# The two meta rows of a projection, as fp32 matmuls on four column tiles of the array

## The chip, the core and the metric

The kernel runs on one core of a Trainium2 chip. The metric is the time of one execution on the device in microseconds (us); lower is better. The core has the matrix engine TensorE (PE in the profile, with its weight loads listed as PEld), the vector engine (DVE), the scalar engine (ACT), GpSimd (POOL) and SyncE (SP), which here issues most DMAs. Each engine works through its own instructions in their order; engines wait for one another by semaphores.

## The reference, cut to what matters

One layer of a hybrid decoder: 1024 tokens of width 1024, with 16 meta tokens put ahead of them. Two branches (attention and convolution) are merged under gates into `mixed`, and the step that the change touches is the product of `mixed` with `w_out` and the normalisation behind it:

```python
mixed = jax.nn.sigmoid(g_attn) * y_attn + jax.nn.sigmoid(g_conv) * y_conv
h = layer_norm(DEEPNORM_ALPHA * h + mixed @ w_out, ln1_g, ln1_b)
up = causal_dwconv(h @ ffn_w_up, ffn_dw, ffn_dw_b)        # 3 taps, causal
...
return h[:, N_META:]
```

Everything is float32. The meta tokens are dropped at the end, but the causal convolution over 3 tokens reads the two tokens ahead of the first real one. So the last two meta rows of `h` are needed, and only these two.

## The kernel before, in words

**Precision.** A float32 product is made of three faster ones in the type `float32r`: each operand is split into a high part, its value in that type, and a low part, what is left. `product` (L340, L343, L344) issues three matmuls per piece of 128 input channels: low x high, high x high, high x low. ACT makes the high parts and DVE the low ones (`split`, L300 and L303).

**The stage around the change.** `w_out` has 8 blocks of 128 rows, k = 0 to 7. `prep_wo` loads a block as float32 (the raw block) and splits it into `wo[k]`, a high and a low part. The raw blocks 0 to 3 lie in the buffer `FA` (columns 2064, 3088, 0 and 1024 on, each 1024 wide), 4 in `FA` from 4112, 5 in `OB` from 3072, and 6 and 7 in `wraw`, a ring of two buffers whose next users are the raw weights `w_up` of the following stage. Once a raw block is split, its place is free.

`out_rows(i)` computes the rows of token tile i (128 tokens): two halves of 512 output columns, 24 matmuls each, into a PSUM tile `ps_w` (tag `mm`, three buffers in turn). DVE adds the residual row, loaded by SP from `h0d` (L1345), collects statistics (L1346) and normalises (L1369). `turn` transposes the rows of an earlier tile on PE (L1379), and ACT writes them scaled into `FA` or, for edge rows, into `edge`. The tiles are taken in the order 3, -1, 7, 2, 6, 0, 4, 1, 5. The tile -1 is the pair of meta rows; the transposes of a tile stand between the halves of the next one, and those of the pair stand after the first half of tile 2.

**The pair.** When the branches are merged, for each block m the two columns of `mixed` that belong to the two meta tokens are written into `pair`: high parts by ACT in `pair[:, m, 0:2]` (L1187), low parts by DVE in `pair[:, m, 2:4]` (L1188). In `out_rows(-1)` each half takes 16 matmuls: per block one with all four columns against the high part of `w_out` (L1356), and one with the two high columns against its low part (L1357). Both add into partitions 0 to 3 of one PSUM tile. ACT copies these four rows out (L1358). Then the rows 2 and 3, which come from the low parts, are moved by a DMA to partitions 0 and 1 and added by DVE (L1364); so are the two residual rows from `h0d` (L1362).

**Order.** A scheduler places every engine's instructions by ranks and by its own estimate of time. `after(a, b)` fixes that a comes behind b in the order of work, without a semaphore. In the kernel before nothing fixes where the pair's matmuls stand; they lie partly between those of tile 3.

Of the kernel before, what the change touches and what calls it, by code (L numbers as in the profile page):

```python
# [23 lines left out]
F = mybir.dt.float32  # L24
R = mybir.dt.float32r
AF = mybir.ActivationFunctionType
OP = mybir.AluOpType
AX = mybir.AxisListType

P = 128  # L30
D = 1024
KC = D // P
# [81 lines left out]
def tile_hybrid_layer(  # L114
# [3 lines left out]
    nc = tc.nc  # L118
# [5 lines left out]
    def load(o, i):  # L124
        return nc.sync.dma_start(out=o, in_=i)
# [5 lines left out]
    def f32(ap):  # L131
        return ap.bitcast(F)

    def after(ins, first):

        tc.add_manual_dep(ins.ins, first.ins.name, mybir.DependencyInfo(
            mybir.DependencyClass.NoSync, mybir.DependencyReason.SCHED_ONLY), reason="order of work")
# [10 lines left out]
    const = ctx.enter_context(tc.tile_pool(name="const", bufs=1, side="left"))  # L148
# [8 lines left out]
    FA = arena.tile([P, 6144], F, name="FA")  # L157
    RHC = arena.tile([P, KC * T], R, name="RHC")
    RHO = arena.tile([P, KC * T], R, name="RHO")
    OB = arena.tile([P, 4 * U], F, name="OB")  # L160
# [8 lines left out]
    h0d = dpool.tile([U, D], F, name="h0d")  # L169
# [11 lines left out]
    start = ExitStack()  # L181
# [30 lines left out]
    tc.cur_priority = RK_START  # L212
    n_right, n_kept = COLS[2][0], COLS[-1][0]
    colr = constr.tile([P, n_right], F, name="colr")
    coll = const.tile([P, n_kept - n_right + 24], F, name="coll")[:, :n_kept - n_right]
    with rank(12):
        load(coll, cols_in[:, n_right:n_kept])
        load(colr, cols_in[:, :n_right])
# [117 lines left out]
    def product(ps, terms, behind=None):  # L336

        n = len(terms)
        for i, (ah, al, bh, bl) in enumerate(terms):
            ins = nc.tensor.matmul(ps, al, bh, start=i == 0, stop=False)  # L340
            if i == 0 and behind is not None:
                after(ins, behind)
            nc.tensor.matmul(ps, ah, bh, start=False, stop=False)  # L343
            last = nc.tensor.matmul(ps, ah, bl, start=False, stop=i == n - 1)  # L344
        return last
# [159 lines left out]
    turned, tms = {}, {}  # L505
# [87 lines left out]
    for a, b in ((0, 400), (400, J_LEN)):  # L593
        ps = pat.tile([P, 512], F, name="ps_v", tag="o" if a == 0 else "mm", bufs=1 if a == 0 else 3)
# [204 lines left out]
    ps = pat.tile([P, 512], F, name="ps_vm", tag="t", bufs=2)  # L799
# [34 lines left out]
    for h in range(NH):  # L834
        g, r = divmod(h, 4)
# [282 lines left out]
    def mixed(i, k, hl):  # L1118
        t, j = MX_AT[i]
        o = j * 2048 + (k * 2 + hl) * P  # L1120
        return t[:, o:o + P]
# [7 lines left out]
        return t[:, 0:8192].rearrange("p (t j x) -> p t j x", t=2, j=2)[:, :, j, cols]  # L1129

    w_out_v = w_out.rearrange("(k p) c -> k p c", p=P)
    wo = {}

    def prep_wo(k, raw=None, behind=None):
        if k < 4:
            hi, lo = (OA[:, OA_WO + k * 2048 + x:OA_WO + k * 2048 + x + 1024] for x in (0, 1024))
        elif k < 6:
            hi, lo = ((RX[:, RX_WO:], RW)[k - 4][:, x:x + 1024] for x in (0, 1024))
        else:
            hi, lo = wsp_flat()  # L1140
        if raw is None:
            raw = wraw([P, D])
            load(raw, w_out_v[k])
        split(raw, hi, lo, behind)
        wo[k] = (hi, lo)

    pair = const.tile([P, KC, 4], R, name="pair")
    g_next = [0]

    GS = [(FA, i * 516) for i in range(4)]  # L1150
# [11 lines left out]
    for m in range(KC):  # L1162
        hi, lo = weights([P, KC, P], lambda raw: load(raw, w_ab[m]))

        def branch(i, g, tag, bufs):
            a, b = PG[g]
            ps = pat.tile([P, 512], F, name="ps_p", tag=tag, bufs=bufs)
            rhs = (oo, conv)[i]
            for k in range(4):
                ah, al = hi[:, 4 * i + k], lo[:, 4 * i + k]  # L1170
                for j, (x, hl) in enumerate(((ah, 0), (ah, 1), (al, 0))):
                    nc.tensor.matmul(ps[:, :b - a], x, rhs(k, hl, a, b), start=k + j == 0, stop=k == 3 and j == 2)  # L1172
            return ps[:, :b - a]

        def merge(g, psa, psb):
            a, b = PG[g]
            n = b - a
            with rank(RK_EVAC):
                t = gslot()[:, :, :n]
                ins = load(t, dram(sgd, m * P * U + a, [[U, P], [KC * P * U, 2], [1, n]]))  # L1180

                ta, tb = t[:, 0], t[:, 1]
                nc.vector.scalar_tensor_tensor(ta, ta, 1.0, psa, OP.add, OP.mult)
                nc.vector.scalar_tensor_tensor(tb, tb, 1.0, psb, OP.add, OP.mult)
                nc.vector.tensor_tensor(ta, ta, tb, OP.add)
                if g == 0:
                    nc.scalar.mul(pair[:, m, 0:2], ta[:, 0:2], 0.5)  # L1187
                    nc.vector.scalar_tensor_tensor(pair[:, m, 2:4], ta[:, 0:2], 0.5, f32(pair[:, m, 0:2]),  # L1188
                                                   OP.mult, OP.subtract)
                v = ta[:, n - 256:].rearrange("p (t x) -> p t x", t=2)  # L1190
                h = mixed2(g, m, 0)
                last_act = nc.scalar.mul(h, v, 0.5)
                nc.vector.scalar_tensor_tensor(mixed2(g, m, 1), v, 0.5, f32(h), OP.mult, OP.subtract)
            return ins, last_act

        if m < KC - 1:
            pa = [branch(0, g, "mm", 3) for g in range(2)]
            for g in range(4):
                if g > 1:
                    pa.append(branch(0, g, "mm", 3))  # L1200
                last_gate, last_act = merge(g, pa[g], branch(1, g, "t", 2))
        else:
            pa = [branch(0, g, "mm", 3) if g < 3 else branch(0, g, "s", 2) for g in range(4)]
            for g in range(4):
                last_gate, last_act = merge(g, pa[g], branch(1, g, "t", 2))
        if m in (2, 3):
            raw = (FA[:, 4112:5136], OB[:, 3072:4096])[m - 2]
            load(raw, w_out_v[m + 2])
            prep_wo(m + 2, raw, last_act)
        if m < 4:  # L1210
            early.append(FA[:, E_AT[m]:E_AT[m] + 1024])
            after(load(early[m], w_out_v[m]), last_gate)
# [104 lines left out]

    WO_ORDER = (4, 5, 0, 1, 2, 3, 6, 7)
    edge = const.tile([P, 2, KC, 2], F, name="edge")
    r_next = [1]  # L1320

    def out_rows(i, between=(), work=()):


        n, u = (P, 2 + i * P) if i >= 0 else (2, 0)
        if n == P:
            o = r_next[0] % 2 * 1024
            r_next[0] += 1
            whole = RT[:, o:o + 1024]
            load(whole, h0d[u:u + n, :])  # L1330
        else:
            whole = OB[:, 3072:4096]
        r = whole[:n]
        order = WO_ORDER if i != 5 else (0, 1, 2, 3, 6, 7, 4, 5)
        turned = None
        st = small.tile([P, 2, 6], F, name="st")
        pin = line if i in (0, 4, 1, 5) else lambda ins: ins
        for half in range(2):
            hs = slice(half * 512, half * 512 + 512)
            ps = pat.tile([P, 512], F, name="ps_w", tag="mm", bufs=3)  # L1340
            if n == P:
                last = product(ps, [(mixed(i, k, 0), mixed(i, k, 1), wo[k][0][:, hs], wo[k][1][:, hs])
                                    for k in order], turned)
                with rank(RK_TURN):
                    pin(nc.vector.tensor_tensor(r[:, hs], ps, r[:, hs], OP.add))  # L1345
                    pin(nc.vector.bn_stats(st[:, half], r[:, hs]))  # L1346
                turned = None
                if len(between) > half:
                    turned = turn(*between[half], behind=[last])
                if half == 0:  # L1350
                    for f, *x in work:
                        f(*x)
                continue

            for j, k in enumerate(order):
                nc.tensor.matmul(ps[:4], pair[:, k], wo[k][0][:, hs], start=j == 0, stop=False)  # L1356
                last = nc.tensor.matmul(ps[:2], pair[:, k, 0:2], wo[k][1][:, hs], start=False, stop=j == KC - 1)  # L1357
            nc.scalar.copy(whole[:4, hs], ps[:4])  # L1358
        if n < P:
            q = FA[:4, 0:1024]  # L1360
            load(q[0:2], h0d[0:2, :])
            nc.vector.tensor_tensor(r, r, q[0:2], OP.add)  # L1362
            load(q[0:2], whole[2:4])
            nc.vector.tensor_tensor(r, r, q[0:2], OP.add)  # L1364
        with rank(RK_TURN):
            (mu, rs), = ln_stats([(r, n)], half_stats=st if n == P else None)
            for a in (512, 0) if i == 5 else (None,):
                x = r if a is None else r[:, a:a + 512]
                ins = pin(nc.vector.tensor_scalar(x, x, mu, rs, OP.subtract, OP.mult))  # L1369
        if n == P:  # L1370
            load(h1d[u - 2:u - 2 + P, :], r)
        return whole, n, ins
# [520 lines left out]
```

## Time and profile before

| | |
|---|---|
| median of 3 runs (lowest to highest) | 1255.88 us (1255.16 to 1256.59) |
| span of the profiled execution, first to last instruction | 1253.2 us |
| time of that execution beyond its span | not given by the profile |
| mean granted TensorE clock | 0.999 |
| matmuls of the pair | 32, from 510.3 to 518.8 us |
| HBM read and written | 150.29 MB and 62.70 MB |

How to read the rows that follow: a timeline row has the start, the duration, the engine, the line of the kernel, the operation, the output and its inputs by the program's names, the shape and the count. For a matmul "128*4 128x512" is the stationary operand (128 rows, 4 columns) and the moving one (128 partitions, 512 elements). Matmuls are pipelined, so durations overlap and their spacing is the difference of two starts. Brackets at the end of a row say how long the engine was idle ahead of it and who released it. A row of a line or tile has the count, then minimum, median and maximum duration in ns, then the first and last start.

### The profile page before, as it was taken

To read this page: it belongs to the slowest core of one execution; us is meant where nothing else is said; L and a number is where in the kernel's file an instruction comes from. 1 tells how busy PE (TensorE), PEld (TensorE's weight loads), DVE (VectorE), ACT (ScalarE), POOL (GpSimd) and SP (SyncE) were. 2 spreads that over 40 slices of the span, in tenths; PEclk is the share of its full clock that TensorE was granted. 3 is DMA by queue.
4 is the path that set the end of the run, shared out by engine and by line. 5 is a ranking of instruction groups with operands and counts; after the bars stand their busy time and mean duration, and the time that the engine had idled before them with its cause. 6 is when DMAs were issued, how large, how long until landed. Compare 5 with 4: busy or idle time off the path is not lost.

```text
span 1253.2 us, 23194 instructions
## 1 busy us (share of the span) xinstructions
PE 1239.1 (99%) x9176; PEld 1173.8 (94%) x9176; DVE 1078.1 (86%) x1862; ACT 627.4 (50%) x1284; POOL 7.4 (1%) x8
## 2 busy tenths in 40 slices
PE   8999999999999999999999999999999999999997
PEld 7999999999999999788899999999999998888886
DVE  8989999999978677448899999998999977896697
ACT  8533255655474233344676556565565654545330
POOL 0000000001000000000000000000000000000000
PEclk9999999999999999999999999999999999999999
DMA  7383633432256564222145555453454567998712
GB/s 261 117 292 102 191 93 98 109 95 81 73 157 173 170 164 119 85 94 75 68 160 191 194 197 201 161 211 137 163 206 175 196 227 251 395 342 330 276 60 84
DMA packets 98687, 212.20 MB, mean 169 GB/s; under 512 B 11395, under 2 KB 38595, under 8 KB 98322
## 3 DMA queue, kind: packets, MB, share of 16 engines
q1 hardware_dynamic: 84414, 199.57, 46.9%
q10 hardware_dynamic: 14164, 11.15, 2.8%
q8 instruction: 72, 1.18, 0.4%
q14 instruction: 37, 0.30, 0.1%
HBM read 150.29 MB, written 62.70 MB: 170 GB/s over the span
## 4 chain that ended last, share of the span: by engine, by line
PE 96%; DVE 2%; ACT 1%; DMA 1%; issue 0%; SPq 0%; DVEq 0%; ACTq 0%
PE px L1594 15%; PE py L1594 10%; PE ps_x L1739 9%; PE ps_z L340 8%; PE ps_z L343 8%; PE ps_z L344 8%; PE ps_z L1739 7%; PE ps_p L1172 7%; PE pz L1594 5%; PE pw L1594 5%; PE ps_w L344 2%; PE ps_w L343 2%; PE ps_w L340 2%; PE ps_z L575 2%; PE ps_t L943 1%; PE ps_s L919 1%
## 5 line engine op out<-in xcount | busy, mean ns | idle before, releaser
L340 PE MATMUL ps_z<-RHO,w 128*128 128x256 f32 (+2 forms) x864 | 243.2, 281 | 0.0
L343 PE MATMUL ps_z<-RHO,w 128*128 128x256 f32 (+2 forms) x864 | 242.3, 280 | 0.0
L344 PE MATMUL ps_z<-RHC,w 128*128 128x256 f32 (+2 forms) x864 | 242.2, 280 | 0.0
L343 PEld LDWEIGHTS ps_z<-RHO,w 128*128 128x128 f32 x864 | 162.5, 188 | 0.5
L344 PEld LDWEIGHTS ps_z<-RHC,w 128*128 128x128 f32 x864 | 162.7, 188 | 0.2
L340 PEld LDWEIGHTS ps_z<-RHO,w 128*128 128x128 f32 x864 | 162.5, 188 | 0.1
L749 DVE SCALAR_TENSOR_TENSOR FA<-cin,cdw,FA 128x1026 f32<-128x1026 f32 x120 | 154.3, 1295 | 0.7
L300 ACT CAST w<-wr 128x1024 fp32r<-128x1024 f32 x37 | 38.8, 1048 | 64.0 <-PE ps_z L344 48.0
L1412 DVE TENSOR_TENSOR RHO<-wr,RHO 128x512 fp32r<-128x512 f32 x94 | 64.0, 684 | 3.6 <-ACT RHO L1411 3.5
L1411 ACT CAST RHO<-wr 128x512 fp32r<-128x512 f32 x94 | 56.9, 619 | 15.6 <-DVE wr L1429 7.9
L1429 DVE TENSOR_TENSOR wr<-wr 128x512 f32<-128x512 f32 x88 | 60.1, 683 | 0.1
L758 ACT ACTIVATE FA<-ps_z,colr 128x258 f32<-128x258 f32 (+1 forms) x64 | 30.1, 472 | 59.0 <-PE ps_z L344 50.7
L303 DVE TENSOR_TENSOR w<-wr,w 128x1024 fp32r<-128x1024 f32 x37 | 45.1, 1218 | 7.6 <-ACT w L300 7.4
L1606 ACT COPY FA<-px 128x516 f32<-128x516 f32 (+2 forms) x23 | 13.1, 571 | 71.2 <-PE px L1594 71.2
L1172 PE MATMUL ps_p<-OC,w 128*128 128x256 f32 (+1 forms) x384 | 48.1, 278 | 0.0
L1172 PE MATMUL ps_p<-OA,w 128*128 128x256 f32 (+1 forms) x384 | 47.8, 278 | 0.0
L1172 PEld LDWEIGHTS ps_p<-OC,w 128*128 128x128 f32 x384 | 46.2, 188 | 0.1
L1172 PEld LDWEIGHTS ps_p<-OA,w 128*128 128x128 f32 x384 | 45.9, 188 | 0.0
L1412 DVE TENSOR_TENSOR w<-wr,w 128x512 fp32r<-128x512 f32 x60 | 40.7, 684 | 4.7 <-ACT w L1411 4.7
L1594 PE MATMUL px<-OA,RHO 128*128 128x260 f32 x324 | 43.0, 282 | 0.0
L1594 PE MATMUL px<-OC,RHO 128*128 128x256 f32 x324 | 41.2, 276 | 0.8 <-DVE OB L1345 0.8
L1594 PE MATMUL px<-RHC,RHO 128*128 128x256 f32 (+1 forms) x312 | 40.6, 279 | 0.1
(457 smaller groups left out, 3109.3 us busy)
## 6 DMA issues: line engine op xcount, KB each, us to landing
wr<-in_w_up_dram SPq DMA_DIRECT2D x44, 512.0 KB, 3.6
wr<-in_w_z_dram SPq DMA_DIRECT2D x29, 512.0 KB, 4.2
OB<-in_w_down_dram SPq DMA_DIRECT2D x24, 512.0 KB, 5.2
fd<-FA SPq DMA_DIRECT2D x44, 256.0 KB, 2.0
FA<-sd SPq DMA_DIRECT2D x15, 512.0 KB, 8.9
qt<-qd SPq DMA_DIRECT2D x28, 256.0 KB, 4.1
OB<-td SPq DMA_DIRECT2D x14, 512.0 KB, 8.7
sgd<-FA ACTq DMA_DIRECT2D x48, 128.0 KB, 2.4
```

The source lines that it names most:

```text
L300: ins = nc.scalar.copy(hi, raw)
L303: return nc.vector.tensor_tensor(lo, raw, f32(hi), OP.subtract)
L340: ins = nc.tensor.matmul(ps, al, bh, start=i == 0, stop=False)
L343: nc.tensor.matmul(ps, ah, bh, start=False, stop=False)
L344: last = nc.tensor.matmul(ps, ah, bl, start=False, stop=i == n - 1)
L749: nc.vector.scalar_tensor_tensor(acc[c], cin[:, j:j + U], wc, acc[c], OP.mult, OP.add)
L1172: nc.tensor.matmul(ps[:, :b - a], x, rhs(k, hl, a, b), start=k + j == 0, stop=k == 3 and j == 2)
L1411: nc.scalar.copy(hi, src)
L1412: ins = nc.vector.tensor_tensor(lo, src, f32(hi), OP.subtract)
L1429: ins = nc.vector.tensor_tensor(*x)
L1594: ins = nc.tensor.matmul(o, (ah, ah, al)[j][:, k * P:(k + 1) * P], bmat(sub, q, j, k), start=first and i == 0, stop=i == 11, skip_group_ch ...
L1739: nc.tensor.matmul(banks[i], l[:, ts], r[:, ws], start=first and a and x + k == 0, stop=z and x == len(ops) - 1 and k == 2, skip_group_che ...
```

## The change

The pair's product is computed from unsplit float32 operands. `pair` becomes a float32 tile of 2 x 8 columns, two per block, followed by 32 columns of zeros. The low parts (L1188) are no longer computed. For block k the stationary operand is the 32 columns from 2k on, of which the first two are the pair's and the rest are not used afterwards; the moving operand is the raw block of `w_out`. Block k writes the partitions from 32 x (k mod 4) on: the four groups of 32 partitions belong to four column tiles of the array, and each of them adds up two blocks. A half takes 8 matmuls, 16 in all. They stand in one row behind tile 3 and ahead of tile 7: each is placed behind the one before by `after`, and so is the first matmul of each token tile's half, unless a transpose stands ahead of it.

ACT copies all 128 partitions out. Then the residual rows and the partial sums in partitions 32, 64 and 96 are moved to partitions 0 and 1 by four DMAs, in two slots of `FA` in turn, and added by four DVE operations. The raw blocks of `w_out` stay in use until the row, so the pair's rows lie in `OB` from 2048 instead of 3072, where raw block 5 is. The padding of `coll` shrinks by as many columns as `pair` grows (16).

```diff
-    coll = const.tile([P, n_kept - n_right + 24], F, name="coll")[:, :n_kept - n_right]
+    coll = const.tile([P, n_kept - n_right + 8], F, name="coll")[:, :n_kept - n_right]
...
-        wo[k] = (hi, lo)
-
-    pair = const.tile([P, KC, 4], R, name="pair")
+        wo[k], wo_raw[k] = (hi, lo), raw
+
+    pair = const.tile([P, 2 * KC + 32], F, name="pair")
+    nc.vector.memset(pair[:, 2 * KC:], 0.0)
...
-                    nc.scalar.mul(pair[:, m, 0:2], ta[:, 0:2], 0.5)
-                    nc.vector.scalar_tensor_tensor(pair[:, m, 2:4], ta[:, 0:2], 0.5, f32(pair[:, m, 0:2]),
-                                                   OP.mult, OP.subtract)
+                    nc.scalar.mul(pair[:, 2 * m:2 * m + 2], ta[:, 0:2], 0.5)
...
-            whole = OB[:, 3072:4096]
+            whole = OB[:, 2048:3072]
...
+                behind = turned or (w_last[-1] if w_last else None)
                 last = product(ps, [(mixed(i, k, 0), mixed(i, k, 1), wo[k][0][:, hs], wo[k][1][:, hs])
-                                    for k in order], turned)
+                                    for k in order], behind)
+                w_last.append(last)
...
-            for j, k in enumerate(order):
-                nc.tensor.matmul(ps[:4], pair[:, k], wo[k][0][:, hs], start=j == 0, stop=False)
-                last = nc.tensor.matmul(ps[:2], pair[:, k, 0:2], wo[k][1][:, hs], start=False, stop=j == KC - 1)
-            nc.scalar.copy(whole[:4, hs], ps[:4])
+            for k in range(KC):
+                o = k % 4 * 32
+                last = nc.tensor.matmul(ps[o:o + 32], pair[:, 2 * k:2 * k + 32], wo_raw[k][:, hs], start=k < 4,
+                                        stop=k >= 4)
+                after(last, w_last[-1])
+                w_last.append(last)
+            nc.scalar.copy(whole[:, hs], ps)
         if n < P:
-            q = FA[:4, 0:1024]
-            load(q[0:2], h0d[0:2, :])
-            nc.vector.tensor_tensor(r, r, q[0:2], OP.add)
-            load(q[0:2], whole[2:4])
-            nc.vector.tensor_tensor(r, r, q[0:2], OP.add)
+            for j, src in enumerate((h0d[0:2, :], whole[32:34], whole[64:66], whole[96:98])):
+                q = FA[:2, j % 2 * 1024:j % 2 * 1024 + 1024]
+                load(q, src)
+                nc.vector.tensor_tensor(r, r, q, OP.add)
```

More of the change, by code (lines that the diff above doesn't have):

```diff
@@ L1131, in tile_hybrid_layer @@
     w_out_v = w_out.rearrange("(k p) c -> k p c", p=P)
-    wo = {}
+    wo, wo_raw = {}, {}
     def prep_wo(k, raw=None, behind=None):
@@ L1319, in tile_hybrid_layer @@
     edge = const.tile([P, 2, KC, 2], F, name="edge")
-    r_next = [1]
+    r_next, w_last = [1], []
     def out_rows(i, between=(), work=()):
```

## The prediction

> **What bounds the kernel now.** I read the busy shares and the chain that ended last on the page, then the waits of PE, then the timeline of PE around the row of the two meta tokens, and last the engines and queues that feed or empty that row.
>
> ```profile
> PE 1239.1 (99%) x9176; PEld 1173.8 (94%) x9176; DVE 1078.1 (86%) x1862; ACT 627.4 (50%) x1284; POOL 7.4 (1%) x8
> PEclk9999999999999999999999999999999999999999
> PE 96%; DVE 2%; ACT 1%; DMA 1%; issue 0%; SPq 0%; DVEq 0%; ACTq 0%
> PE pw L1594 <- ACT FA L1392: 1.2, 1, 1.2
> PE px L1594 <- DVE OB L1345: 0.8, 1, 0.8
> 620.00:900.00 280.00, 280.00 (x2415) 280.00 (x2414) 262.03 (x421) 171.50 (x369) 0.00 (x0) 1.00 0.49 177
> ```
>
> TensorE (PE) is busy for 99% of the span at the full granted clock and carries 96% of the chain. The two wait rows are all that PE waits for after 506 us: 2.0 us, both on the last token tile, whose date is set by PE itself. The windows row (PE, PEld, DVE, ACT, POOL busy, then clock and DMA) shows the next stage: DVE is nearly full, 262 of 280 us, but PE does not wait for it. So what PE gains or loses in the changed row should reach the end one for one, unless a feeder of that row turns late.
>
> The row itself, in the timeline (start, duration, engine, line):
>
> ```profile
> 510.05 0.39 PE L344 MATMUL ps_w<-w,RHC 128*128 128x512 f32 x1
> 510.27 0.40 PE L1356 MATMUL ps_w<-RX,pair 128*4 128x512 f32 x1
> ...
> 513.05 0.39 PE L1356 MATMUL ps_w<-OA,pair 128*4 128x512 f32 x1
> ...
> 518.84 0.40 PE L1357 MATMUL ps_w<-w,pair 128*2 128x512 f32 x1
> 519.08 0.40 PE L340 MATMUL ps_w<-RX,RHC 128*128 128x512 f32 x1
> ...
> 524.56 1.03 PE L1379 MATMUL ps_h<-coll,OB 128*128 128x128 f32 x8
> 510.05:519.08 9.03, 7.75 (x32) 2.70 (x32) 0.00 (x0) 0.00 (x0) 1.00 0.29 107
> ```
>
> Durations overlap, so cost is read from start to start. From 513.05 to 519.08 there are 26 matmuls of the row in 6.03 us, 0.232 us each. From 519.08 to 524.56 there are the 24 matmuls of half a token tile in 5.48 us, 0.228 us each. The last line is the window cut to the tile `pair`: all 32 matmuls of the row start in it, and seven of token tile 3 besides. **Removed: 32 x 0.232 = 7.42 us** of PE; the seven belong to tile 3 and stay.
>
> **The change part by part.** *The new matmuls.* Sixteen fp32 matmuls, stationary 32 columns, moving 512 columns; the trace has no fp32 matmul on several column tiles, but it has fp32 matmuls:
>
> ```profile
> L572 PE MATMUL ps_z<-FA,wr x32: 392/393/497, 12.6 to 21.2; 128*128 128x272 f32 x32
> 15.89 5.67 PE L572 MATMUL ps_z<-FA,wr 128*128 128x272 f32 x24
> 21.40 0.82 PE L518 MATMUL ps_h<-coll,xn 128*128 128x128 f32 x6
> 8.33 0.09 PEld L595 LDWEIGHTS ps_v<-tab 128*8 128x8 f32 x1 [0.25 <-issue]
> 8.66 0.09 PEld L595 LDWEIGHTS ps_v<-tab 128*8 128x8 f32 x1 [0.24 <-issue]
> ```
>
> The code issues 16 matmuls at L572, and the trace has 32: each fp32 matmul is **two passes**, one right behind the other on the same part of the array. 24 passes of 272 columns take 21.40 - 15.89 = 5.51 us, 0.2296 us each, or 0.844 ns per column; the passes of 400 columns at L595 (8 stationary columns) are 0.33 us apart, 0.83 ns per column. The present row needs 0.232 / 512 = 0.45 ns. So a pass over 512 columns is an estimated 512 x 0.844 = **0.432 us**, and 16 matmuls have 32 of them. What that costs hangs on how many run side by side; no row shows that, so I bound it:
>
> - nothing overlaps: 32 x 0.432 = 13.8 us, +6.4 us against 7.42;
> - all four tiles run at once: 8 x 0.432 = 3.5 us, -4.0 us;
> - between them: tiles are independent, but passes start in the order of the program. The order is tile 0 first pass, tile 0 second pass, tile 1 first pass, and so on. Tile 0's second pass must wait for its first, and tile 1's first pass stands behind it. It then starts beside it. Two passes run at any time, each matmul costs one pass, and the row is 17 x 0.432 = 7.35 us, **-0.1 us**.
>
> I take the last one: the timeline of PE nowhere shows a matmul overtaking another, and L572 shows the two passes as neighbours. The Trainium skill, "TensorE: Matmul & The Clock Gate", section Part 3, says that matmuls keep program order in start and end and only weight loads are pulled ahead. The trace agrees as far as one tile goes (510.27 to 518.84 in steps of 0.23); no run here shows several.
>
> *Weight loads.* 32 loads of 4 or 2 columns become 32 of 32 columns:
>
> ```profile
> L1356 PEld LDWEIGHTS ps_w<-OA,pair x8: 84/84/84, 511.9 to 517.5; 128*4 128x4 f32 x8
> L863 PEld LDWEIGHTS ps_pm<-coll,pm x36: 108/110/113, 176.5 to 328.2; 128*64 128x64 f32 x36
> ```
>
> Between 84 and 110 ns each. Beside a pass of 0.432 us they are hidden if a tile's load may run under another tile's pass (0). If only one load can be ahead at a time, tile 1's load waits until tile 0's second pass has begun, and each matmul takes 0.432 + 0.10: 16 x 0.53 + 0.43 = 8.9 us, +1.5 us. I take 0, since in the row of now all loads are hidden, and keep +1.5 for the range.
>
> *The evacuation and the longer sum.* Where one load and two adds follow the row now, four loads on SP (one of them from `h0d`) and four adds follow, and each slot of `q` is used twice.
>
> ```profile
> 519.27 0.57 ACT L1358 COPY OB<-ps_w 4x512 f32<-4x512 f32 x1 [1.52 <-PE ps_w L1357]
> 521.12 0.70 SPq L125 DMA_DIRECT2D FA<-OB  x1
> 523.19 1.21 DVE L1364 TENSOR_TENSOR OB<-OB,FA 2x1024 f32<-2x1024 f32 x1 [2.09 <-DMA FA<-OB]
> 525.64 0.66 DVE L1345 TENSOR_TENSOR OB<-ps_w,OB 128x512 f32<-128x512 f32 x1
> 529.91 0.28 ACT L271 ACTIVATE sd<-mv,eps 2x1 f32<-2x1 f32 x1
> 531.70 0.79 DVE L1369 TENSOR_SCALAR OB<-OB,mv,sd 2x1024 f32<-2x1024 f32 x1
> 542.68 0.60 PE L1379 MATMUL ps_h<-coll,OB 128*128 128x128 f32 x4
> ```
>
> The copy moves 512 elements per partition either way, 0.57 us. After it two more rounds of a load (521.12 to 523.19, 2.1 us) and an add (1.21 us) are needed, and they pair up in two slots: the last add ends near 526.7 instead of 524.4, +2.3 us. The root at 529.91 stands behind ACT's work for tile 3 anyway, and PE transposes the row only at 542.68, while it is ready at 532.5. That slack of 10 us hides it; without it the cost would be 2.3 us once. What stands behind the waiting adds on DVE is tile 7's first evacuation (525.64); its PSUM bank is one of three and is wanted about two half tiles (11 us) later. Cost 0. DVE loses eight splits:
>
> ```profile
> L1188 DVE SCALAR_TENSOR_TENSOR pair<-OB,pair x7: 152/161/161, 428.7 to 500.5; 128x2 fp32r<-128x2 f32 x7
> ```
>
> 8 x 0.16 = 1.3 us off an engine that PE does not wait for: 0 at the end; the `memset` of `pair` is off the path too.
>
> *Raw weights held longer.* The fp32 product reads the raw rows of `w_out`, so their buffers come free only after the row. Two are the ring `wraw`, so both loads of `w_up` for the next stage move behind it; two are the slots of `q`.
>
> ```profile
> 508.30 0.33 SPq L125 DMA_DIRECT2D wr<-in_w_up_dram  x1
> 508.74 0.37 SPq L125 DMA_DIRECT2D OB<-h0d  x1
> ...
> 525.63 0.34 SPq L125 DMA_DIRECT2D OB<-h0d  x1
> L1411 ACT CAST RHO<-wr x10: 605/642/674, 564.3 to 631.0; 128x512 fp32r<-128x512 f32 x10
> 513.59 1.29 DVE L1345 TENSOR_TENSOR OB<-ps_w,OB 128x512 f32<-128x512 f32 x2 [4.99 <-DMA OB<-h0d]
> 518.37 0.81 DVE L1369 TENSOR_SCALAR OB<-OB,mv,sd 128x1024 f32<-128x1024 f32 x1
> ```
>
> The first reader of those `w_up` rows is at 564.3, some 45 us after the row: 0, if nothing urgent stands behind them on SP. The load of 525.63 does; it serves the half tile two halves after the evacuation at 525.64, about 11 us later, and takes under 5 (508.74 to 513.59). Hidden. The seven matmuls of tile 3 that now stand between those of the row come ahead of it, up to 1.4 us earlier than today; the load of 508.30 could start because the last split of `w_out` had ended, so their operands are there: 0.
>
> **Sum:** -0.1 (matmuls) + 0 + 0 + 0 = -0.1 us, 1253.1 us of span. The profile gives the span, 1253.2 us, and no total for that execution; the median of the runs is 2.7 us above the span, which I leave as it is: 1255.88 - 0.1 = **1255.8 us**.
>
> **The rivals.**
>
> *Four tiles at once.* If a pass that waits for its own tile does not hold up the next tile, the row is 3.5 us and the kernel gains 4.0: 1251.9 us. For it: the four tiles have separate stationary columns and separate PSUM partitions, and accumulate apart. Against it: the adjacent passes of one tile. The Trainium skill, "TensorE: Matmul & The Clock Gate", section Part 3, measured three column tiles of 32 at 2.38 times the speed of one; by that share of the ideal the row would be an estimated 13.8 / 3.2 = 4.3 us and the kernel 1252.8. No run so far shows it.
>
> *No overlap: slower.* Passes on different column tiles take turns, as the passes at L572 do on one tile. The place is the row itself, the price 32 x 0.432 - 7.42 = +6.4 us: 1262.3 us. It decides as soon as on average fewer than 13.8 / 7.42 = 1.9 passes run side by side. For it: every neighbouring pair of matmuls in the trace takes turns. Against it: all those pairs share their columns, so the trace never tried.
>
> *SP blocked: slower.* If the order on SP keeps the `w_up` load (508.30) ahead of tile 3's load from `h0d` (508.74), that load waits for the end of the row, near 519.1, and lands 4.9 us later (508.74 to 513.59), at 524.0. Tile 3's chain on DVE (513.59 to 519.18, 5.6 us) then ends at 529.6, and PE stands at tile 3's transposes from 524.56: +5.0 us, 1260.9 us. Against it: the loads on SP now stand in the order in which their buffers came free, which puts `w_up` behind.
>
> **How the numbers follow.** Two passes at a time, with loads hidden or not: 0.50. Four at once or close to it: 0.28. No overlap: 0.14. SP blocked, or another wait of that kind: 0.08. A measurement of this kernel can tell about 0.2%, 2.5 us, from no change. The first case lies within it; of the second nearly all is faster (0.26) and the rest same; the last two are slower, 0.22. The range takes in the first two, 0.78: from 1251.9 less 0.7 us for the runs' own scatter, to 1255.88 + 1.5 + 0.7. That is 1251.2 to 1258.1 us. The first case alone would be 1255.1 to 1258.1.
>
> **What would show it.** Right: 32 passes in the row, starting two by two some 0.43 us apart, about 7.4 us from the first to the first matmul of tile 7; no new wait of PE; `w_up` loads near 519. Wrong: four starts together and a row of 3.5 to 4.3 us; single starts 0.43 apart and a row of 13.8 us; PE idle ahead of L1379 for tile 3; or a loss that sits outside the row, which none of my terms holds.

## The result and the profile after

| | median | runs |
|---|---|---|
| before, beside the changed kernel | 1254.4 us (1253.57 to 1256.59) | 18 |
| changed | 1252.18 us (1250.92 to 1254.21) | 18 |

The ratio is 0.9979 (95% interval 0.9973 to 0.9985): **2.6 us faster** (1.9 to 3.4). The profiled execution of the changed kernel took 1251.86 us, with a span of 1250.1 us; 1.8 us lie around the span. The first three runs of the kernel before were high: with 18 its median is 1254.4, not 1255.88. The ratios here and below are those on record with the runs. They are not the quotients of the medians (here 0.9982), so the gains that go with them differ somewhat from the differences of the medians (here 2.2 us).

The page of the changed kernel, busy shares and the chain that ended last, and one row of its waits of PE:

```profile
PE 1236.5 (99%) x9176; PEld 1172.2 (94%) x9176; DVE 1079.4 (86%) x1857; ACT 627.6 (50%) x1284; POOL 7.4 (1%) x8
PE 91%; DVE 5%; DMA 2%; ACT 1%; issue 1%; SPq 0%; DVEq 0%; ACTq 0%
...
PE ps_z L1742 <- DVE RHC L1692: 0.2, 1, 0.2
```

PE still bounds the kernel. The share of PE in the chain has fallen from 96% to 91%, but not at the change. It falls between 990 and 1060 us, in the last stages: PE waits 0.2 us for DVE there, at 1059.80 us, and from this wait the chain is followed back through DVE and DMAs. One wait of 0.2 us moves the share by five points, so the share says little here; in free3_both, below, it is 96% again. The PE timeline of the changed kernel, from the end of tile 3's first half to the first matmuls of tile 7 (brackets: idle ahead of the row, and who ended it):

```profile
504.21 0.40 PE L344 MATMUL ps_w<-w,RHC 128*128 128x512 f32 x1
504.85 0.50 PE L340 MATMUL ps_w<-w,RHC 128*128 128x512 f32 x1 [0.25 <-ACT w L300]
505.19 0.40 PE L343 MATMUL ps_w<-w,RHC 128*128 128x512 f32 x1
506.11 0.50 PE L344 MATMUL ps_w<-w,RHC 128*128 128x512 f32 x1 [0.53 <-DVE w L303]
...
511.69 0.39 PE L344 MATMUL ps_w<-w,RHC 128*128 128x512 f32 x1
512.01 1.48 PE L1358 MATMUL ps_w<-FA,pair 128*32 128x512 f32 x9
512.90 0.59 PE L1358 MATMUL ps_w<-OB,pair 128*32 128x512 f32 x1
512.90 0.60 PE L1358 MATMUL ps_w<-wr,pair 128*32 128x512 f32 x2
513.32 0.59 PE L1358 MATMUL ps_w<-FA,pair 128*32 128x512 f32 x1
...
515.05 0.60 PE L1358 MATMUL ps_w<-wr,pair 128*32 128x512 f32 x2
515.58 0.50 PE L340 MATMUL ps_w<-RX,RHC 128*128 128x512 f32 x1
515.92 0.39 PE L343 MATMUL ps_w<-RX,RHC 128*128 128x512 f32 x1
```

Two things are to be seen. The row runs from 512.01 to 515.58, **3.57 us** where it took 7.42: `FA` holds the raw blocks 0 to 4, `OB` block 5 and `wr` blocks 6 and 7, and the rows show block 5 and blocks 6 and 7 starting at the same time, with the next group 0.42 us behind. So four passes run side by side. And ahead of it, inside tile 3's first half, PE has two waits that were not there: 504.21 to 504.85 and 505.19 to 506.11, for the two parts of the last split of `w_out`.

From here I compare stretches rather than end times, since the profiles differ by chance at the start of the kernel. Before the change does anything, tile 3's first matmul starts at 497.88 us in the profile of before, at 496.80 in that of the changed kernel, and between 496.76 and 498.31 in those below. The stretch from there to the transposes of tile 7 holds all that the change touches:

| kernel | row of the pair | tile 3's first matmul to tile 7's first | transposes of tile 3 to those of tile 7 | first matmul of tile 3 to transposes of tile 7 | against before |
|---|---|---|---|---|---|
| before | 7.42, partly among tile 3 | 21.20 | 11.77 | 38.45 | |
| changed | 3.57 | 18.78 | 11.77 | 36.13 | -2.32 |
| order_only | 7.40 | 22.56 | 11.77 | 39.81 | +1.36 |
| one_tile | 13.85 | 29.05 | 11.77 | 46.40 | +7.95 |
| by_tile | 3.61 | 18.81 | 12.81 | 37.24 | -1.21 |
| free3 | 3.57 | 17.42 | 13.10 | 36.10 | -2.35 |
| free3_slots | 3.57 | 17.42 | 11.77 | 34.77 | -3.68 |
| free3_late_w | 3.57 | 17.42 | 11.77 | 34.78 | -3.67 |
| free3_both | 3.57 | 17.42 | 11.77 | 34.77 | -3.68 |
| free3_one_add | 3.57 | 17.43 | 11.77 | 34.78 | -3.67 |

The 7.42 us of before are 32 matmuls of 0.232 us; the other rows are measured from the first matmul of the pair to the first of tile 7. The row gains 7.42 - 3.57 = 3.85 us. The stretch gains 2.32, near the 2.6 us of the runs. The question is where the other 1.5 us went.

### The profile page after: what moved, and what is told of

It reads as the page before. It is cut to its first block, busy times and chain, and to the rows that moved or that the text cites. A ratio compares the mean times of both kernels' runs of the same rounds, so it can differ in the third digit from the quotient of the medians.

```text
span 1250.1 us, 23200 instructions
## 1 busy us (share of the span) xinstructions
PE 1236.5 (99%) x9176; PEld 1172.2 (94%) x9176; DVE 1079.4 (86%) x1857; ACT 627.6 (50%) x1284; POOL 7.4 (1%) x8
## 4 chain that ended last, share of the span: by engine, by line
PE 91%; DVE 5%; DMA 2%; ACT 1%; issue 1%; SPq 0%; DVEq 0%; ACTq 0%
PE px L1597 13%; PE ps_x L1742 9%; PE py L1597 8%; PE ps_z L340 8%; PE ps_z L343 8%; PE ps_z L344 8%; PE ps_p L1173 7%; PE ps_z L1742 5%; PE pz L1597 4%; PE pw L1597 4%; PE ps_w L344 2%; PE ps_w L340 2%; PE ps_w L343 2%; PE ps_z L575 2%; PE ps_t L943 1%
## 5 line engine op out<-in xcount | busy, mean ns | idle before, releaser
L1414 ACT CAST w<-wr 128x512 fp32r<-128x512 f32 x60 | 36.2, 619 | 8.9 <-DMA wr<-in_w_up_dram 4.7
```

The lines of the kernel that those rows point to most:

```text
L1414: nc.scalar.copy(hi, src)
```

## The experiments

My theory after the result (A) was: the four tiles each have a queue of their own, so the row gains 3.85 us, and the fixed order that came with it gives back 1.3 us in tile 3. Against it stood B, that later stages swallow the difference, and C, that the order gains and the tiles do little.

### free3: tile 3's two halves unbound

```diff
-                behind = turned or (w_last[-1] if w_last else None)
+                behind = turned or (w_last[-1] if i != 3 else None)
...
-                after(last, w_last[-1])
+                for x in w_last[-2:] if k == 0 else w_last[-1:]:
+                    after(last, x)
```

> The changed kernel, but the two halves of tile 3 may be interleaved again; the row of the pair stays behind both. Theory A: the row on four tiles saves 7.42 - 3.57 = 3.85 us, and about 1.3 us of it is given back because the fixed order makes PE wait inside tile 3's first half for the last split of w_out (two waits, 0.25 and 0.53 us, and the slow starts around them). Then both waits vanish, the stretch from tile 3's first matmul to tile 7's first takes 18.8 - 1.3 = 17.5 us, and the kernel is about 1.3 us faster than the changed one, 3.5 to 3.9 us faster than before. Rival B: the missing microsecond is lost after the row, in the later stages; then the waits go but the time stays at that of the changed kernel, 2.6 us under before.

Measured: 1252.4 us beside 1254.46, ratio 0.9981 (0.9971 to 0.9990). No faster than the changed kernel, which is what B said. But the profile says something else. The waits of PE between 490 and 600 us, and the PE timeline at the transposes of tiles 3 and 7:

```profile
PE ps_h L1383 <- issue: 1.2, 1, 1.2
```

```profile
519.93 1.03 PE L1383 MATMUL ps_h<-coll,OB 128*128 128x128 f32 x8
...
533.03 1.06 PE L1383 MATMUL ps_h<-coll,OB 128*128 128x128 f32 x8 [1.17 <-issue]
```

Both waits for the split are gone and the stretch to tile 7 is 17.42 us, as A had it. In their place stands a new one: 13.10 us instead of 11.77 between the transposes. What I gained at tile 3 PE lost again ahead of tile 7's transposes, so A was right about the loss in tile 3 and missed a second limit just behind it. The DVE timeline of free3 shows it:

```profile
522.53 2.46 DVE L1368 TENSOR_TENSOR OB<-OB,FA 2x1024 f32<-2x1024 f32 x2 [1.71 <-DMA FA<-OB]
525.91 1.21 DVE L1368 TENSOR_TENSOR OB<-OB,FA 2x1024 f32<-2x1024 f32 x1 [0.92 <-DMA FA<-OB]
...
528.96 0.66 DVE L1346 TENSOR_TENSOR OB<-ps_w,OB 128x512 f32<-128x512 f32 x1
...
532.12 0.81 DVE L1373 TENSOR_SCALAR OB<-OB,mv,sd 128x1024 f32<-128x1024 f32 x1
```

The adds of the pair's four sums (L1368) stand in DVE's order ahead of tile 7's second evacuation (L1346) and wait for their loads. Tile 7's rows are normalised (L1373) only at 532.93, and the transposes start 0.1 us later. The profile calls the idle time "issue", since it does not see the releaser there; the DVE row names it.

### order_only: the kernel before with the order alone

```diff
                 last = product(ps, [(mixed(i, k, 0), mixed(i, k, 1), wo[k][0][:, hs], wo[k][1][:, hs])
-                                    for k in order], turned)
+                                    for k in order], turned or (w_last[-1] if w_last else None))
+                w_last.append(last)
...
+                    after(x, w_last[-1])
+                    w_last.append(x)
```

(x is each of the pair's 32 `float32r` matmuls in turn.)

> The kernel before with only the order of the change: tile 3's halves, then the pair's 32 float32r matmuls in one row, then tile 7. Theory A: the row stays at 7.4 us, the two waits of PE for the split appear, and the kernel is 0.8 to 1.4 us slower than before. Rival C: the order itself is what gains (a row in one piece, no changes between narrow and full matmuls); then it is 1 to 3 us faster than before, and the four tiles bring little.

Measured: 1256.48 us beside 1254.46, ratio 1.0012 (1.0003 to 1.0021), 1.5 us **slower** (0.4 to 2.6). The waits of PE between 490 and 530 us:

```profile
PE ps_w L344 <- DVE w L303: 0.5, 1, 0.5
PE ps_w L340 <- ACT w L300: 0.2, 1, 0.2
```

They are the two of the changed kernel, and the stretch is 1.36 us longer than before. C has fallen: the order costs. In the kernel before, tile 3's second half could go on where its first half lacked the split of block 7; in a fixed order it can't.

### one_tile: all 16 matmuls on one column tile

```diff
-                o = k % 4 * 32
+                o = 0
...
-            nc.scalar.copy(whole[:, hs], ps)
+            nc.scalar.copy(whole[:32, hs], ps[:32])
...
-            for j, src in enumerate((h0d[0:2, :], whole[32:34], whole[64:66], whole[96:98])):
+            for j, src in enumerate((h0d[0:2, :],)):
```

> The changed kernel with all 16 fp32 matmuls on the first column tile, in the same order; the three adds of the other tiles' sums fall away, the sum is the same. Theory A: nothing runs side by side, 32 passes of 0.43 us, a row of 13.7 to 13.8 us instead of 3.57, and the kernel is 10.2 us slower than the changed one, 7.6 us slower than before: what PE loses reaches the end one for one. Rival B (later stages take up part of what PE gains or loses): the row is as long, but the kernel loses clearly less than 10 us.

Measured: 1264.51 us beside 1254.46, ratio 1.0073 (1.0060 to 1.0087), 9.2 us slower (7.5 to 10.9). The PE timeline:

```profile
513.51 4.48 PE L1358 MATMUL ps_w<-FA,pair 128*32 128x512 f32 x10
517.83 1.02 PE L1358 MATMUL ps_w<-OB,pair 128*32 128x512 f32 x2
518.68 1.88 PE L1358 MATMUL ps_w<-wr,pair 128*32 128x512 f32 x4
520.40 4.46 PE L1358 MATMUL ps_w<-FA,pair 128*32 128x512 f32 x10
...
527.36 0.50 PE L340 MATMUL ps_w<-RX,RHC 128*128 128x512 f32 x1
```

Sixteen passes from 513.51 to 520.40 are 0.431 us each: the size of a pass was right, and so was the price of no overlap, a row of 13.85 us. Four tiles are 13.85 / 3.57 = 3.9 times as fast as one. The stretch is 7.95 us longer than before, which lies within the interval of the runs, so what PE loses here arrives at the end; B is refuted for a loss. Whether the 1.2 us between 7.95 and 9.2 mean anything is left open: PE waits 1.1 us for ACT in the last stage of this profile alone, and nothing shows whether that belongs to the delay.

### by_tile: two blocks of one tile behind one another

```diff
-            for k in range(KC):
+            for k in (0, 4, 1, 5, 2, 6, 3, 7):
                 o = k % 4 * 32
```

> The changed kernel with the blocks in the order 0, 4, 1, 5, 2, 6, 3, 7, so that two matmuls, four passes, stand behind one another on the same tile. Queue theory D: every tile has its own queue, deep enough for all; the row stays at 3.6 us and the time at that of the changed kernel. Weight theory E: a matmul may wait at its tile without holding up the next, but a weight load must find a free place, one ahead per tile, and loads keep their order; then the next tile's loads stand behind the fourth load of this one, each tile adds 2 passes and a load, 0.96 us, and the row is about 8.5 us, +4.9 us. Order theory F, my prediction's: a waiting pass holds up all behind it; three passes per tile are alone, the row is about 10.8 us, +7.2 us.

Measured: 1253.58 us beside 1254.46, ratio 0.9991 (0.9982 to 1.0000); the row takes 3.61 us. Its weight loads and the first of its passes in the timeline:

```profile
512.55 0.18 PEld L1358 LDWEIGHTS ps_w<-FA,pair 128*32 128x32 f32 x8 [0.35 <-issue]
513.01 0.11 PEld L1358 LDWEIGHTS ps_w<-FA,pair 128*32 128x32 f32 x1 [0.28 <-issue]
513.02 0.11 PEld L1358 LDWEIGHTS ps_w<-OB,pair 128*32 128x32 f32 x1
513.03 0.12 PEld L1358 LDWEIGHTS ps_w<-wr,pair 128*32 128x32 f32 x2
...
512.55 1.47 PE L1358 MATMUL ps_w<-FA,pair 128*32 128x512 f32 x9
513.45 0.59 PE L1358 MATMUL ps_w<-OB,pair 128*32 128x512 f32 x1
```

Block 4 stands second in the program. Its tile is busy, so its first load comes at 513.01, together with those of 5, 6 and 7; the eight loads at 512.55 are both passes of blocks 0 to 3, and three of these four blocks stand behind block 4. The nine passes of the row at 512.55 are the eight of these blocks and block 4's first, which ends the row and so starts near 513.43 (512.55 + 1.47 - 0.59), beside that of block 5. So D holds in what it says of the row: neither a waiting pass nor a waiting load holds up another tile, four passes deep. E and F, my prediction's, have fallen: 8.5 and 10.8 us were due. The time did not stay at the changed kernel's, though: this kernel has the stall at tile 7's transposes too, 1.04 us in the table, where its pair's loads came late.

### Two ways out of the stall, and the sum left out

Four more kernels, all built on free3. free3_slots gives the third load a slot of its own:

```diff
-                q = FA[:2, j % 2 * 1024:j % 2 * 1024 + 1024]
+                q = OB[:2, 3072:4096] if j == 2 else FA[:2, j % 3 * 1024:j % 3 * 1024 + 1024]
```

> free3 with a slot of its own (a part of OB) for the third of the four loads of the pair's sum, so that no load waits for an add just done. In free3 PE stood 1.2 us at the transposes of tile 7 (533.03). Theory G: DVE takes its work in order, and the pair's last adds, waiting for their loads, stand ahead of tile 7's evacuation and normalisation, so these end after 532.9 instead of by 531.7. With three loads in flight at once the wait of 0.92 us for the last one goes; the stall falls to 0.3 us or less, and the kernel is about 1 us faster than free3. Rival H: the stall has another cause (tile 7's own load, ACT); then it stays at 1.2 us and so does the time.

free3_late_w puts the first two loads of `w_up` behind the pair's loads:

```diff
-                load(q, src)
+                q_last.append(load(q, src))
...
-            load(raw, w_up[m].rearrange("p k c -> p (k c)"))
+            ins = load(raw, w_up[m].rearrange("p k c -> p (k c)"))
+            if c == 0:
+                after(ins, q_last[-1])
```

> free3 with the two loads of w_up (512 KB each, issued at 514.5 to 515.7, just ahead of the pair's small loads at 516.9 to 518.6) placed behind the pair's last load. Theory I: the small loads land late because the big ones go ahead of them on the same DMA engines; then they land about 2.1 us after their issue as in the kernel before, the first add behind them starts near 521 instead of 522.53, the stall at tile 7's transposes shrinks by about 1.2 us to nothing, and the kernel is 1 us or more faster than free3. Rival: small loads in slots used twice take this long anyway; then the add at 522.5 and the stall stay.

free3_both has both edits:

> Both together. Theories G and I: no stall at tile 7's transposes, 11.77 us from the transposes of tile 3 to those of tile 7 as in the kernel before; the gain of the row arrives whole: 3.85 us against before, about 1250.6 us where before is 1254.4, and 1.3 to 1.6 us faster than the changed kernel. Rival B: it stays at the time of the changed kernel, 0.998 of before.

free3_one_add leaves the three partial sums out, with their loads and adds, so that the pair's rows hold the blocks 0 and 4 only:

```diff
-            for j, src in enumerate((h0d[0:2, :], whole[32:34], whole[64:66], whole[96:98])):
+            for j, src in enumerate((h0d[0:2, :],)):
```

> free3 without the three partial sums of the other column tiles: their loads and adds are left out, so the pair's rows hold the blocks 0 and 4 only. Theory G: nothing of the pair holds up DVE, no stall at tile 7's transposes, 11.77 us between the transposes, the time is that of free3_both (3.5 to 4 us under before). If the stall of 1.2 us stays, the sum of four is not its cause.

| kernel | median | before beside it | ratio (95% interval) |
|---|---|---|---|
| free3_slots | 1250.82 us | 1254.63 us | 0.9970 (0.9959 to 0.9981) |
| free3_late_w | 1250.92 us | 1254.63 us | 0.9971 (0.9960 to 0.9982) |
| free3_both | 1250.31 us | 1254.63 us | 0.9969 (0.9957 to 0.9981) |
| free3_one_add | 1251.75 us | 1254.63 us | 0.9980 (0.9970 to 0.9991) |

In all four the transposes of tile 7 follow those of tile 3 after 11.77 us and the stall is gone, so G holds and H has fallen. For I, first free3 (its SP queue), then free3_late_w (its SP queue, then its DVE):

```profile
514.46 1.26 SPq L125 DMA_DIRECT2D wr<-in_w_up_dram  x2
516.56 0.33 SPq L125 DMA_DIRECT2D h1d<-OB  x1
516.94 1.69 SPq L125 DMA_DIRECT2D FA<-OB  x2
```

```profile
515.76 0.69 SPq L125 DMA_DIRECT2D FA<-OB  x1
516.71 0.34 SPq L125 DMA_DIRECT2D h1d<-OB  x1
517.83 1.81 SPq L125 DMA_DIRECT2D FA<-OB  x2
519.69 0.87 SPq L125 DMA_DIRECT2D wr<-in_w_up_dram  x2
```

```profile
516.60 2.45 DVE L1368 TENSOR_TENSOR OB<-OB,FA 2x1024 f32<-2x1024 f32 x2
519.81 2.46 DVE L1368 TENSOR_TENSOR OB<-OB,FA 2x1024 f32<-2x1024 f32 x2 [0.76 <-DMA FA<-OB]
```

With the two loads of 512 KB ahead of them, the small loads issued from 516.94 on let DVE go on at 522.53; with the big ones behind, the first one, issued at 515.76, is there for the second of the two adds that start at 516.60, and the last add starts near 521.0 instead of 525.91. I expected the adds near 521 and they came earlier, since the first small load is also issued 1.2 us earlier. The rest is a faster load: from the issue to the add that waits for it, a small load took 5.6 us in free3 (516.94 to 522.53) and 2.0 us in free3_late_w (517.83 to 519.81). By what the big loads slow the small ones is not shown, and the delay is not the same each time. free3_slots has the big loads ahead too, and there (its SP queue, then its DVE) the same small load is read by its add 3.8 us after the issue:

```profile
517.06 0.68 SPq L125 DMA_DIRECT2D FA<-OB  x1
```

```profile
520.87 1.20 DVE L1368 TENSOR_TENSOR OB<-OB,FA 2x1024 f32<-2x1024 f32 x1
```

So in free3_slots the wait of 1.71 us ahead of the second add is gone as well as the one of 0.92 us, and a slot for the third load explains the latter alone. That the stall goes when the adds end earlier is shown; how much the slot itself does is not.

free3_one_add has the stretch of the other three (34.78 us), but its median lies 1 us above theirs; the intervals overlap, and its profiled execution took 1251.12 us. I read its profile, not its median, as the answer on the stall; that its time is that of free3_both, as I expected, is not shown.

**free3_both is faster than before by 3.9 us** (2.4 to 5.4), against 2.6 us (1.9 to 3.4) for the change as it was. The two intervals overlap, so the ratios alone don't show that it beats the changed kernel; the traces do for the stretch, which is 1.36 us shorter (34.77 against 36.13). That free3_slots or free3_late_w alone is worse than both together is not shown.

## Why the prediction was right, and where it was wrong

The time lay in the range, and near the rival "four tiles at once" (1251.9 us, 4.0 us of gain) rather than at the forecast of no change. The range held because it was made to take in that rival; the mechanism that the forecast took was the wrong one. That 1252.18 lies so near 1251.9 is luck besides: the rival started from a median 1.5 us too high (1255.88 for 1254.4), and its gain was 1.4 us more than the 2.6 measured. Point by point:

- **What bounds the kernel: right.** PE's loss and gain in the stretch reached the end: +1.36 became +1.5 (order_only), -3.68 became -3.8 and -3.9 (free3_slots, free3_both).
- **Size of a pass: right.** 0.432 us from the 272-column passes; 0.431 measured at 512 columns.
- **Passes side by side: wrong, and the largest error.** The step that failed is "Tile 0's second pass must wait for its first, and tile 1's first pass stands behind it." by_tile shows that nothing stands behind a waiting pass but its own tile's work. The bound of four tiles, 3.5 us, was the row; 3.57 measured. I had an argument from rows in which all neighbours shared their columns and, as I wrote, "the trace never tried" the other case; it deserved less than 0.50. The Trainium skill, "TensorE: Matmul & The Clock Gate", section Part 3, has matmuls start and end in program order; by_tile disagrees for passes on different column tiles, as block 1's loads and first pass come ahead of block 4's. The same section gives three column tiles 2.38 times the speed of one; here four gave 3.9.
- **Tile 3 in one piece: wrong by 1.36 us.** I wrote that "their operands are there: 0", and looked only at the seven matmuls of tile 3 at the row (six stand between its matmuls; the seventh, at 510.05, stands ahead of them). The edit binds every half behind the one before, so tile 3's second half could no longer fill PE while its first half lacked the split of block 7. It is the main part of what was given back.
- **The longer sum and the raw weights: no cost in the changed kernel's profile, but the cover was far thinner than I said.** I gave the pair's row 10 us of slack and asked of what stands behind the adds only when its PSUM bank is wanted. The nearer reader is the transpose of tile 7. Before, and then in the changed kernel, the DVE row that ends its normalisation and the PE row that reads it:

```profile
534.28 0.81 DVE L1369 TENSOR_SCALAR OB<-OB,mv,sd 128x1024 f32<-128x1024 f32 x1
536.33 1.03 PE L1379 MATMUL ps_h<-coll,OB 128*128 128x128 f32 x8
```

```profile
525.78 1.22 DVE L1367 TENSOR_TENSOR OB<-OB,FA 2x1024 f32<-2x1024 f32 x1 [1.36 <-DMA FA<-OB]
...
532.00 0.81 DVE L1372 TENSOR_SCALAR OB<-OB,mv,sd 128x1024 f32<-128x1024 f32 x1
532.93 1.04 PE L1382 MATMUL ps_h<-coll,OB 128*128 128x128 f32 x8
```

  1.24 us were left before (535.09 to 536.33), 0.12 are left now (532.81 to 532.93), and about 0.1 of that is the handover itself: in free3, where PE does wait, it starts 0.10 us behind this row (532.93 to 533.03). That is why the next 1.36 us, won back in free3, stopped there. The term itself was mis-sized too. I had +2.3 us for the longer sum; the last add ends 11.4 us behind the row (515.58 to 527.00) where it ended 5.3 us behind it before (519.08 to 524.40), 6.1 us more. I had placed the `w_up` loads behind the row rightly (515.99 us) and asked what stands behind them on SP; the pair's own loads do.
- **No overlap and SP blocked:** the first didn't come, and its price was right (13.8 and 13.85 us). For the second, SP took tile 3's load ahead of `w_up`, as argued.

So the sum of the change, by measured terms: -3.85 for the row, +1.36 for the order, +0.2 left over, which is the size of the slower steps into the row and behind tile 7's first matmul (0.09 and 0.11 us, at the end of this document); -2.3 us in the stretch, -2.6 (1.9 to 3.4) in the runs.

## What to carry to other kernels

When an order is fixed by hand to keep one row together, look at every pair that it binds, not only at what stood between: a list that was free to interleave was hiding a late operand, and it showed at once as a wait. When a transfer chain grows and "has slack", walk the in-order queue behind its waiting instructions to the nearest reader on the bound engine; the slack that counts is that reader's. And an end time that does not move says little by itself: free3's time was that of the changed kernel while one wait had been exchanged for another, and only a stretch by stretch comparison showed it.

## What the runs showed of the hardware

Two-pass fp32 matmuls on four column tiles of 32 run side by side almost perfectly: 32 passes of 512 columns in 3.57 us, or 3.61 us in the other order of the blocks, against 13.85 us on one tile. Each tile takes its passes and weight loads in its own order, and in by_tile four passes deep. Around the row PE loses about 0.3 us in all: 0.32 us instead of 0.23 at the first matmul of the row (511.69 to 512.01), 0.11 us behind the last pass (515.05 + 0.42 to 515.58), and 0.34 instead of 0.23 behind the first matmul of tile 7 (515.58 to 515.92). The row of 4 and 2 columns in the kernel before showed no such gaps. Whether the column tiles cost this, or the type of the operands, or something else, is not shown: a first step of 0.32 us also stands behind the transposes on 128 columns in the kernel before (525.35 to 525.67).
